# Tiles turned by one engine or another, GpSimd instructions of 256 columns, and who makes the lower parts during a tree of decays

## The chip, the cores and the metric

The program runs on one core of a Trainium2 chip. A core has TensorE (PE, matmuls and its weight loads, PEld), VectorE (DVE), ScalarE (ACT), GpSimd (POOL), and queues that move data; SyncE (SP) issues nearly all loads here. The metric is the device time of one launch, in microseconds (us). Engines execute their instructions in the order in which the program lists them, each waiting for the semaphores that its operands need.

## The reference, cut to what matters

Two layers. Each has two token mixers that run side by side and are merged (HGRN2, a gated recurrence, and stick-breaking attention), then a PEER layer: 8 heads choose 16 of 16,384 one-neuron experts for each of 256 tokens.

```
proj = (x * (1 + sc1) + sh1) @ w_in[l]
oa = hgrn2(qa, fa, ia)          # S_t = diag(f_t) S_{t-1} + (1 - f_t) outer v_t, o_t = S_t^T q_t
ob = stick_breaking_attention(qb, kb, vb)
merged = sigmoid(gate_a) * (norm(oa) * silu(ga) @ w_up_a[l]) + sigmoid(gate_b) * (ob @ w_up_b[l])
y = (merged @ w_o[l]) * gt1
x = layer_norm(DN_ALPHA * x + y, ln_g[l, 0], ln_b[l, 0])
hf = x * (1 + sc2) + sh2
idx, gates = product_key_top16(hf @ w_pq[l], sub_keys[l])
act = gelu(hf . peer_u[l][idx])
y = (sum over k of gates * act * peer_v[l][idx]) * gt2
x = layer_norm(DN_ALPHA * x + y, ln_g[l, 1], ln_b[l, 1])
```

The kernel computes the product of hf with all 16,384 rows of peer_u, and the product of the (mostly zero) gate matrix with all rows of peer_v.

## The kernel before

**Split products.** Every matrix that TensorE multiplies is split into an upper part (`wh`, rounded by ScalarE, the helper at L58) and a lower part (`wl` = raw minus wh, the subtraction at L271), and a product is three matmuls: upper by upper, upper by lower, lower by upper (the helper at L61). A tile of weights is 128 x 1024 numbers, so it has two upper halves and two lower halves of 512 columns each. `fetch` issues a load, `turn` does what a tile needs ahead of the split, `prep` splits it, `take` hands the oldest split tile to the matmuls and prepares the next. Instructions are listed in the order in which this Python code runs.

**Who makes the lower halves.** `lighter` keeps an estimate of the work listed on VectorE and GpSimd and picks the one with less for tiles of kind "w" (outside slabs) and "o"; expert tiles ("u", "x") have theirs on GpSimd (flag `pool_lo`/kind) while selection runs.

**Turning expert tiles.** The rows of `peer_u` have to stand with the model dimension on the partitions. A "u" tile is loaded by four DMAs in blocks of 32 and turned by one VectorE transpose of blocks (L220). An "x" tile is turned by eight TensorE transposes of 128x128 into PSUM (L251), from which ScalarE writes both the upper part and the plain copy. The table `uv_seq` (L124) makes every fourth tile with j under 100 an "x" tile.

**Stages of a layer.** Mixers, merge, layer norm, queries for PEER, then 126 tiles of `peer_u` (U stage) with the selection of the experts running beside them, then `peer_v` (V stage). In the U stage `pull(sides, budget)` lists a share of the selection's operations after each tile, by costs that the generators yield: `scores` and top-16 searches on VectorE, with the scores made by transposes and products on TensorE into the tile `G` and copied to SBUF by ScalarE (`buf<-G`).

**The tree over time.** `hgrn()` computes the recurrence over 256 steps as a tree of 9 levels (`sizes`). For a level `st_exp` lists two VectorE subtractions (L843, L844) and ScalarE's exponential, `st_mul` two VectorE products into `qk` (L856, L857), `st_score` TensorE's products (`hs`, `ss`), and `st_place` VectorE's masked copies into `sc` (L887). Between two levels a tile of weights for the projections is split and multiplied.

**Start of layer 1.** `make_masks()` (L684 and the lines around it) and `update_x()`, which finishes the layer norm of layer 0 by multiplying x by a row and adding one on GpSimd (L698, L702), run beside the first projections. In layer 0 the modulation sums `mh` (L381, L1143) stand there.

**The merge.** In the merge of the two mixers, tiles of w_o ("o") are scaled on GpSimd by `gt_row` in `turn` (L223), and VectorE adds the two gated parts (L1281 to L1283) and makes lower halves.

## Time and profile before

| | us |
|---|---|
| median of 3 runs | 2228.16 (2227.01 to 2228.52) |
| the profiled execution's own time | 2227.97 |
| its span in the trace | 2226.2 |
| PE busy | 2117.0 (95%) |
| DVE busy | 1819.4 (82%) |
| ACT busy | 1164.5 (52%) |
| POOL busy | 1063.8 (48%) |

The span is the time between the first and the last instruction in the trace; 1.8 us of the execution lie around it. Busy shares are means over stages with different limits. Layer 0 has its mixers in the first 300 us or so and its U stage from about 320 to 770; layer 1 starts near 1150 and has its U stage from about 1412 to 1862. In a row of a timeline, "x8" merges eight instructions in a row, the first number is the start, the second the time from the first start to the last end, and the bracket tells how long the engine was idle before it and what ended that.

### The profile page before, as it was taken

How to read it: one execution, taken by the hardware profiler on the slowest of the kernel's cores; microseconds unless marked ns; L12 is line 12 of the kernel's file. 1: busy time of each engine (PE TensorE's matmuls, PEld its weight loads, DVE VectorE, ACT ScalarE, POOL GpSimd, SP SyncE). 2: the span in 40 equal slices, each digit the busy share in tenths (PEclk: the TensorE clock that was granted, in tenths of full speed). 3: DMA queues.
4: the chain of work that ended last, by engine and by line, in shares of the span. 5: the costliest groups of instructions: out<-in, count | busy, mean ns of one | idle time of the engine just before them, and what ended most of it. 6: DMA issues, size and time to landing. Idle time of an engine off the chain costs nothing.

```text
span 2226.2 us, 42039 instructions
## 1 busy us (share of the span) xinstructions
PE 2117.0 (95%) x14484; PEld 1928.0 (87%) x14484; DVE 1819.4 (82%) x3296; ACT 1164.5 (52%) x2443; POOL 1063.8 (48%) x784
## 2 busy tenths in 40 slices
PE   5799899999999999999989998998999999999998
PEld 5789799999999977888779887998999999788886
DVE  7887979999999578888887658789999985766675
ACT  3446555545554545555545465555555545555562
POOL 4656637887778621000044534578877783300001
PEclk8899999999999999999999999999999999999999
DMA  8646567676665678888844335676766556666662
GB/s 281 193 133 221 167 132 158 149 151 146 143 147 146 186 251 270 282 283 284 298 153 146 120 103 146 149 155 142 154 146 145 147 159 192 220 196 191 197 226 87
DMA packets 448718, 400.30 MB, mean 180 GB/s; under 512 B 234576, under 2 KB 395896, under 8 KB 448504
## 3 DMA queue, kind: packets, MB, share of 16 engines
q1 hardware_dynamic: 446760, 392.33, 62.5%
q0 software_dynamic: 1408, 4.23, 0.6%
q8 instruction: 114, 1.87, 0.3%
q10 hardware_dynamic: 336, 1.06, 0.1%
q14 instruction: 100, 0.82, 0.1%
HBM read 396.46 MB, written 1.05 MB: 179 GB/s over the span
## 4 chain that ended last, share of the span: by engine, by line
PE 69%; DVE 15%; DMA 5%; issue 3%; ACT 3%; POOL 2%; SPq 1%; POOLq 0%; ACTq 0%; DVEq 0%
PE Y L61 27%; PE A L61 25%; PE T L61 7%; PE G L61 3%; DMA raw<-in_peer_u_dram 3%; POOL wl L271 2%; PE hs L61 2%; DVE wl L271 2%; PE ss L61 2%; PE T L251 2%; DMA raw<-in_peer_v_dram 1%; DVE qk L857 1%; DVE o L1512 1%; SPq L197 1%; DVE e L843 1%
## 5 line engine op out<-in xcount | busy, mean ns | idle before, releaser
L271 POOL TENSOR_TENSOR wl<-raw,wh 128x512 fp32r<-128x512 f32 x663 | 925.7, 1421 | 662.0 <-ACT wh L58 587.3
L58 ACT ACTIVATE wh<-raw 128x512 fp32r<-128x512 f32 x1088 | 627.7, 622 | 206.8 <-PE A L61 59.0
L61 PE MATMUL A<-hTh,wh 128*128 128x256 f32 x2080 | 538.5, 291 | 2.7 <-ACT wh L58 2.6
L61 PE MATMUL A<-hTl,wh 128*128 128x256 f32 x2080 | 521.0, 283 | 0.0
L61 PE MATMUL Y<-wh,o 128*128 128x512 f32 x1776 | 478.1, 391 | 0.5 <-DVE o L521 0.5
L271 DVE TENSOR_TENSOR wl<-raw,wh 128x512 fp32r<-128x512 f32 x525 | 379.7, 764 | 64.0 <-ACT wh L58 46.4
L61 PEld LDWEIGHTS A<-hTh,wh 128*128 128x128 f32 x2080 | 397.8, 191 | 4.7 <-ACT wh L58 4.0
L61 PEld LDWEIGHTS A<-hTl,wh 128*128 128x128 f32 x2080 | 398.7, 192 | 0.7
L61 PEld LDWEIGHTS Y<-wh,o 128*128 128x128 f32 x1776 | 332.6, 188 | 70.0 <-DVE o L521 0.9
L61 PE MATMUL A<-hTh,wl 128*128 128x256 f32 x2080 | 336.2, 284 | 13.5 <-POOL wl L271 13.4
L61 PEld LDWEIGHTS A<-hTh,wl 128*128 128x128 f32 x2080 | 286.9, 192 | 17.6 <-POOL wl L271 17.6
L61 PE MATMUL Y<-wl,o 128*128 128x512 f32 x888 | 276.3, 391 | 5.2 <-DVE wl L271 5.0
L220 DVE STREAM_TRANSPOSE raw<-raw 128x1024 f32<-128x1024 f32 x206 | 252.8, 1233 | 3.2 <-DMA raw<-in_peer_u_dram 2.7
L58 ACT ACTIVATE o<-buf 128x256 fp32r<-128x256 f32 x228 | 95.0, 417 | 272.6 <-PE Y L61 272.6
L521 DVE TENSOR_TENSOR o<-buf,o 128x256 fp32r<-128x256 f32 x228 | 100.7, 442 | 140.2 <-ACT o L58 140.2
L61 PEld LDWEIGHTS Y<-wl,o 128*128 128x128 f32 x888 | 167.1, 188 | 44.0 <-DVE wl L271 9.5
L58 ACT ACTIVATE buf<-G 128x128 f32<-128x128 f32 (+6 forms) x236 | 53.8, 273 | 202.7 <-PE G L61 202.7
L1507 DVE TENSOR_TENSOR o<-iT,iota_t 128x1024 f16<-128x1024 f16 x128 | 159.5, 1246 | 0.0
L570 POOL TENSOR_TENSOR x<-x,buf 128x1024 f32<-128x1024 f32 x1 | 2.4, 2392 | 280.9 <-DVE x L567 280.9
L1512 DVE TENSOR_TENSOR o<-gT,o 128x1024 f16<-128x1024 f16 x128 | 131.3, 1025 | 4.4
L61 PE MATMUL T<-hTh,wh 128*128 128x256 f32 x512 | 133.8, 293 | 0.0
L61 PE MATMUL T<-hTl,wh 128*128 128x256 f32 x512 | 130.4, 287 | 0.0
(496 smaller groups left out, 3212.6 us busy)
## 6 DMA issues: line engine op xcount, KB each, us to landing
raw<-in_peer_u_dram SPq DMA_DIRECT2D x1024, 128.0 KB, 3.5
raw<-in_peer_v_dram SPq DMA_DIRECT2D x256, 512.0 KB, 4.6
raw<-in_w_in_dram SPq DMA_DIRECT2D x88, 512.0 KB, 4.7
raw<-in_w_ada_dram SPq DMA_DIRECT2D x78, 512.0 KB, 4.9
raw<-in_w_o_dram SPq DMA_DIRECT2D x16, 512.0 KB, 3.5
raw<-in_w_pq_dram SPq DMA_DIRECT2D x64, 128.0 KB, 2.9
qk<-in_w_ada_dram SPq DMA_DIRECT2D x10, 512.0 KB, 3.7
e<-in_w_ada_dram SPq DMA_DIRECT2D x8, 512.0 KB, 6.0
```

Of the source, the lines that this page charges most:

```text
L58: nc.scalar.activation(o, i, f, **kw)
L61: nc.tensor.matmul(o, a, b, start=start, stop=stop, **kw)
L197: nc.sync.dma_start(dst[32 * b:32 * b + 32], src[b])
L220: nc.vector.transpose(t, t)
L251: nc.tensor.transpose(banks[s][:, q], t[:, (4 * s + q) * P:(4 * s + q + 1) * P], ident)
L271: eng.tensor_sub(lo, src, h.bitcast(F32))
L521: nc.vector.tensor_sub(lo, src, h.bitcast(F32))
L570: nc.gpsimd.tensor_mul(xt[tt], xt[tt], last[0])
L843: eng.tensor_sub(ev[:, :, :hn], mid, bv[:, :, :hn])
L857: nc.vector.tensor_mul(tv[:, :, hn:], nodes(qT, n)[:, :, hn:], ev[:, :, hn:])
L1507: nc.vector.tensor_tensor(o.rearrange("p a u n v -> p (a u) n v"), iT[:, b].rearrange("p a (u v) -> p (a u) v", v=2)[:, :, None] .to_broad ...
L1512: nc.vector.tensor_mul(og.rearrange("p u a n v -> p (u a) n v"), gT[:, b * nu:(b + 1) * nu].rearrange("p u a v -> p (u a) v")[:, :, None] ...
```

## The change

Three things change.

First, an "x" tile now needs 24 <= j < 100, so j = 3, 7, 11, 15, 19 and 23 of each layer become "u" tiles: other DMAs, one VectorE transpose in place of eight of TensorE, and one ScalarE pass over the tile in place of two. In the first 24 tiles the budget of `pull` is 1.75 after every tile; before it was 1.55, and 2.75 after an "x" tile.

Second, GpSimd's 128x512 subtractions for tiles other than "u" and "x" become two of 256 columns, its multiply of an "o" tile by `gt_row` four of 256 (counted as 2.9 in the planner's estimate, before 2.4), and the four 128x1024 operations of `update_x` sixteen of 256, with one listed for each step of the side work.

Third, from the start of `hgrn()` to the end of its loop over levels, a flag makes VectorE do every lower half that GpSimd might have got, without adding it to the planner's estimate.

```diff
-    uv_seq = [("x" if j % 4 == 3 and j < 100 else "u", j) for j in range(NK)] + [("v", j) for j in range(NK)]
+    uv_seq = [("x" if j % 4 == 3 and 24 <= j < 100 else "u", j) for j in range(NK)] + [("v", j) for j in range(NK)]
...
             elif kind == "o" and state.get("gt_row") is not None:
-                nc.gpsimd.tensor_mul(t, t, state["gt_row"])
-                load["pool"] += 2.4
+                for c in range(0, 1024, 256):
+                    nc.gpsimd.tensor_mul(t[:, c:c + 256], t[:, c:c + 256], state["gt_row"][:, c:c + 256])
+                load["pool"] += 2.9
                 fetched[i] = ("ot", t)
...
             else:
-                eng = lighter(0.6, 1.0) if kind == "o" or kind == "w" and not state.get("slab") else nc.vector
-            eng.tensor_sub(lo, src, h.bitcast(F32))
+                eng = nc.vector if state.get("vector_lo") else lighter(0.6, 1.0) if kind == "o" or kind == "w" and not state.get("slab") else nc.vector
+            if kind not in "ux" and eng is nc.gpsimd:
+
+                for c in (slice(0, 256), slice(256, 512)):
+                    eng.tensor_sub(lo[:, c], src[:, c], h[:, c].bitcast(F32))
+            else:
+                eng.tensor_sub(lo, src, h.bitcast(F32))
...
-                for tt in range(2):
-                    nc.gpsimd.tensor_mul(xt[tt], xt[tt], g_row)
-                    load["pool"] += 2.4
-                    yield None
-                    yield None
-                    nc.gpsimd.tensor_add(xt[tt], xt[tt], b_row)
-                    load["pool"] += 2.4
-                    yield None
+                for n in range(16):
+                    cs = slice(n % 4 * 256, n % 4 * 256 + 256)
+                    xc = xt[n // 8][:, cs]
+                    (nc.gpsimd.tensor_add if n // 4 % 2 else nc.gpsimd.tensor_mul)(
+                        xc, xc, (b_row if n // 4 % 2 else g_row)[:, cs])
+                    load["pool"] += 0.7
                     yield None
...
+                state["vector_lo"] = True
                 sc0 = ap.tile([P, HG_H, S], F32, name="sc0")
...
+                state["vector_lo"] = False
                 fine[0] = l == 1
...
-                    pull(sides, 1.55 + 1.2 * (kind == "x"))
+                    pull(sides, 1.75 if j < 24 else 1.55 + 1.2 * (kind == "x"))
```

Lines from L223 on have other numbers in the changed file: the subtraction at L271 is L277 (in pieces, L275), L843/L844 are L849/L850, L856/L857 are L862/L863, L887 is L893, L698/L702 are L706, and the row loads at L434 are L440.

On VectorE, in one level of the tree of layer 1, before (two exponent subtractions, two masked copies, two products, and the next level's subtractions):

```order
L843 TENSOR_TENSOR e<-bb 128x128x4
L844 TENSOR_TENSOR e<-bb 128x128x4
L887 COPY_PREDICATED sc_14338<-masks,hs 128x4x4x16
L887 COPY_PREDICATED sc_14339<-masks,ss 128x16x16
L856 TENSOR_TENSOR qk<-kk,e 128x128x4
L857 TENSOR_TENSOR qk<-qT,e 128x128x4
```

and one level in the changed kernel:

```order
L849 TENSOR_TENSOR e<-bb 128x32x16
L850 TENSOR_TENSOR e<-bb 128x32x16
L277 TENSOR_TENSOR wl<-raw,wh 128x512 x2
L893 COPY_PREDICATED sc_14403<-masks,hs 128x4x64
L893 COPY_PREDICATED sc_14404<-masks,ss 128x4x64
L862 TENSOR_TENSOR qk<-kk,e 128x32x16
L863 TENSOR_TENSOR qk<-qT,e 128x32x16
```

Two lower halves now stand on VectorE between the level's subtractions and its copies and products. On ScalarE, at the same place of the changed kernel, the order is as before: the level's exponential, then the two upper halves that those lower halves are made from.

```order
L58 ACTIVATE e<-e 128x1024
L58 ACTIVATE wh<-raw 128x512 x2
L58 ACTIVATE sc_14403<-hs 128x4x128
L58 ACTIVATE e<-e 128x1024
L58 ACTIVATE wh<-raw 128x512 x2
```

Nothing moved on ScalarE there. On GpSimd, at the start of layer 1, before (`mh` are the two rows of the layer norm):

```order
L434 DMA mh_13854<-in_ln_g_dram 128x1024
L434 DMA mh_13855<-in_ln_b_dram 128x1024
L271 TENSOR_TENSOR wl<-raw,wh 128x512 x2
L698 TENSOR_TENSOR x_79<-x_79,mh_13854 128x1024
L271 TENSOR_TENSOR wl<-raw,wh 128x512
L702 TENSOR_TENSOR x_79<-x_79,mh_13855 128x1024
L271 TENSOR_TENSOR wl<-raw,wh 128x512
```

and in the changed kernel:

```order
L440 DMA mh_13897<-in_ln_g_dram 128x1024
L440 DMA mh_13898<-in_ln_b_dram 128x1024
L275 TENSOR_TENSOR wl<-raw,wh 128x256 x4
L706 TENSOR_TENSOR x_79<-x_79,mh_13897 128x256
L275 TENSOR_TENSOR wl<-raw,wh 128x256 x2
L706 TENSOR_TENSOR x_79<-x_79,mh_13897 128x256
L275 TENSOR_TENSOR wl<-raw,wh 128x256 x2
```

The same data pass through GpSimd in quarters and halves, and one quarter of an x operation now alternates with one 512-column half made of two pieces.

On TensorE, in the first 24 expert tiles, eight transposes stand between the products of two tiles before:

```order
L61 MATMUL A<-hTh,wl 128x256 x4
L61 MATMUL K<-buf_3125,buf_3124 128x256
L251 MATMUL T<-ident,raw 128x128 x8
L61 MATMUL A<-hTh,wh 128x256
L61 MATMUL A<-hTl,wh 128x256
```

In the changed kernel the row of eight transposes is gone there, six times in each layer; the first one stands after tile 24. VectorE has a transpose of its own in their place.

## Rows read from the trace of the kernel before

**Rows 1.** Busy time of each engine in stretches: the first 80 us of the U stage of layer 0, a later part of it, and the first 80 us of the U stage of layer 1. The columns are the stretch, its length, then for PE, PEld, DVE, ACT and POOL the busy us with the number of instructions, the granted TensorE clock, DMA share and GB/s.

```profile
322.70:402.60 79.90, 79.90 (x652) 79.05 (x651) 69.48 (x371) 46.25 (x102) 60.17 (x49) 1.00 0.72 158
475.00:690.00 215.00, 213.64 (x1989) 208.88 (x1988) 210.27 (x303) 118.30 (x312) 166.55 (x118) 1.00 0.64 148
1416.40:1496.30 79.90, 79.90 (x652) 79.06 (x651) 69.48 (x371) 46.25 (x102) 60.16 (x49) 1.00 0.72 158
```

**Rows 2.** What VectorE waits for in the first stretch of rows 1: total us, times, longest.

```profile
DVE buf L1404 <- ACT G L58: 10.4, 8, 2.4
```

**Rows 3.** The timeline of TensorE at one "x" tile of that stretch.

```profile
342.33 1.03 PE L251 MATMUL T<-ident,raw 128*128 128x128 f32 x8
343.12 0.36 PE L61 MATMUL A<-hTh,wh 128*128 128x256 f32 x1
```

**Rows 4.** VectorE's transposes in that stretch, by line: count, busy us, mean ns.

```profile
L220 DVE STREAM_TRANSPOSE raw<-raw 128x1024 f32<-128x1024 f32 x17 | 21.0, 1238 | 0.0
```

**Rows 5.** The timeline of VectorE in one level of the tree of layer 1.

```profile
1228.65 0.68 DVE L844 TENSOR_TENSOR e<-bb 128x512 f32<-128x512 f32 x1
1229.26 0.43 DVE L887 COPY_PREDICATED sc<-masks,hs 128x256 f32<-128x256 uint8 x1
1229.59 0.44 DVE L887 COPY_PREDICATED sc<-masks,ss 128x256 f32<-128x256 uint8 x1
1230.52 0.69 DVE L856 TENSOR_TENSOR qk<-kk,e 128x512 f32<-128x512 f32 x1 [0.49 <-ACT e L58]
1231.13 1.79 DVE L857 TENSOR_TENSOR qk<-qT,e 128x512 f32<-128x512 f32 x1
1232.84 1.75 DVE L843 TENSOR_TENSOR e<-bb 128x512 f32<-128x512 f32 x1
1234.51 0.68 DVE L844 TENSOR_TENSOR e<-bb 128x512 f32<-128x512 f32 x1
```

**Rows 6.** ScalarE in the same level.

```profile
1229.43 1.06 ACT L58 ACTIVATE e<-e 128x1024 f32<-128x1024 f32 x1 [3.29 <-DVE e L844]
1230.39 1.14 ACT L58 ACTIVATE wh<-raw 128x512 fp32r<-128x512 f32 x2
```

**Rows 7.** GpSimd in the same level.

```profile
1231.09 2.96 POOL L271 TENSOR_TENSOR wl<-raw,wh 128x512 fp32r<-128x512 f32 x2 [2.90 <-ACT wh L58]
```

**Rows 8.** VectorE in level 0 of the tree of layer 0: a modulation sum.

```profile
107.16 1.28 DVE L381 SCALAR_TENSOR_TENSOR acc<-raw,cond,acc 128x1024 f32<-128x1024 f32 x1
```

**Rows 9.** What TensorE waits for in the tree of layer 0 and, below it, in that of layer 1: total us, times, longest.

```profile
PE hs L61 <- DVE qk L857: 11.9, 7, 6.5
...
PE hs L61 <- DVE qk L857: 7.7, 7, 1.8
```

**Rows 10.** GpSimd over the whole run by line and shape: the product with gt_row, and the only form of 256 columns.

```profile
L223 POOL TENSOR_TENSOR raw<-raw,gt_row 128x1024 f32<-128x1024 f32 x16 | 43.0, 2694 | 3.0 <-DVE gel L1283 1.6 <-DVE v_a L271 1.3
L1737 POOL TENSOR_TENSOR x<-x,buf 128x256 f32<-128x256 f32 x32 | 30.6, 991 | 4.7 <-DMA buf<-in_ln_b_dram 4.7
```

**Rows 11.** GpSimd at the start of layer 1.

```profile
1159.03 2.55 POOL L271 TENSOR_TENSOR wl<-raw,wh 128x512 fp32r<-128x512 f32 x2
1163.60 2.41 POOL L698 TENSOR_TENSOR x<-x,mh 128x1024 f32<-128x1024 f32 x1 [2.02 <-DMA mh<-in_ln_g_dram]
```

**Rows 12.** VectorE at the start of layer 1: operations on the masks, then lower halves.

```profile
1158.16 3.46 DVE L684 TENSOR_TENSOR m_a<-m_a,m_b 128x4 f32<-128x4 f32 x1
...
1162.20 0.17 DVE L684 TENSOR_TENSOR m_a<-m_a,m_b 128x8 f32<-128x8 f32 x1
...
1163.74 2.32 DVE L684 TENSOR_TENSOR m_a<-m_a,m_b 128x32 f32<-128x32 f32 x1
...
1167.20 2.38 DVE L682 TENSOR_SCALAR m_a<-iota_f,part_f 128x64 f32<-128x64 f32 x1
...
1170.18 3.70 DVE L271 TENSOR_TENSOR wl<-raw,wh 128x512 fp32r<-128x512 f32 x6
```

**Rows 13.** TensorE at the start of layer 1.

```profile
1170.93 1.23 PE L61 MATMUL T<-hTh,wl 128*128 128x256 f32 x4 [4.87 <-DVE wl L271]
```

**Rows 14.** VectorE at the start of layer 0: eight modulation sums, and eight again with GpSimd idle.

```profile
41.49 5.28 DVE L381 SCALAR_TENSOR_TENSOR mh<-e,cond,mh 128x256 f32<-128x256 f32 x8
...
61.43 3.25 DVE L381 SCALAR_TENSOR_TENSOR mh<-e,cond,mh 128x256 f32<-128x256 f32 x8
```

**Rows 15.** GpSimd at the start of layer 0.

```profile
43.64 4.26 POOL L271 TENSOR_TENSOR wl<-raw,wh 128x512 fp32r<-128x512 f32 x3 [2.11 <-ACT wh L58]
...
54.50 6.34 POOL L271 TENSOR_TENSOR wl<-raw,wh 128x512 fp32r<-128x512 f32 x5
```

**Rows 16.** VectorE in the merge of layer 1.

```profile
1341.26 2.89 DVE L1283 TENSOR_TENSOR gel<-gel,mgb 128x512 f32<-128x512 f32 x1
...
1349.37 2.89 DVE L1283 TENSOR_TENSOR gel<-gel,mgb 128x512 f32<-128x512 f32 x1
1352.18 3.45 DVE L271 TENSOR_TENSOR wl<-raw,wh 128x512 fp32r<-128x512 f32 x2
```

**Rows 17.** What TensorE waits for: at the start of layer 0, in the merge of layer 0, and in the merge of layer 1.

```profile
PE ss L61 <- DVE mh L1143: 8.5, 2, 4.4
...
PE T L61 <- DVE wl L271: 2.4, 2, 1.8
...
PE T L61 <- DVE wl L271: 4.9, 2, 2.8
```

## The prediction

> **What bounds the kernel now.** I read the busy shares first: PE works 95% of the span, so most of the time is matmul work that the change leaves alone, and a gain has to come out of the few stretches in which PE waits, or out of work taken from PE. Then I read windows. In the first 80 us of the U stage PE has no gap at all, 79.90 of 79.90 us, while DVE is busy 69.48 [rows 1]; DVE's 10.4 us of idle there are one wait, for ScalarE's copy of scores that PE makes in its turn [rows 2]. So there DVE waits for PE. Later in the stage PE has 213.64 of 215.00 us and DVE 210.27 [rows 1], so both are close to full. In the two trees over time it is the other way round: PE waits 11.9 and 7.7 us for VectorE's products [rows 9]. At the start of layer 0 PE waits 8.5 us for modulation sums, at the start of layer 1 4.87 us for a lower half, and in the merges 2.4 and 4.9 us for lower halves [rows 13, 17]. All of these last waits are on DVE. The sum goes against the profiled execution, 2227.97 us, 0.19 below the median.
>
> **A, the tiles not turned by TensorE.** Six tiles a layer lose eight transposes each. From their start to that of the next matmul is 343.12 - 342.33 = 0.79 us [rows 3], so PE loses 6 x 0.79 = 4.7 us a layer, in a stretch where it sets the pace; 79.9 becomes 75.2. DVE gains 6 x 1.238 = 7.4 us [rows 4]. The budget of the side work in these 24 tiles goes from 24 x 1.55 + 6 x 1.2 = 44.4 to 24 x 1.75 = 42.0, so 2.4 us of selection leave the stretch. DVE is then busy 69.48 + 7.4 - 2.4 = 74.5 us of 75.2. That fits only if its wait of 10.4 us [rows 2] shrinks to 0.7. It should shrink nearly so: DVE waits since it is ahead of PE, and a slower DVE with a faster PE is less ahead. Of 4.7 I count 4.0 as gained. The 2.4 us that are moved later meet a DVE that is nearly full [rows 1]. Most of the stage after them has PE in front, and the selection ends some tiles before the U stage does, so I charge 0.7 and not 2.4. That leaves 3.3 a layer. Layer 1's stretch reads the same to 0.01 us [rows 1], so A is -6.6. Bounds: -9.4 (all of 2 x 4.7) and 0, where the moved work and the waits eat it; the case beyond 0 is the first rival. The loads are four DMAs of 128 KB a tile in either kind, on the same queue, with a DMA share of 0.72 in the stretch [rows 1], and ScalarE, 46.25 us busy of 79.9, loses a pass: both at nothing, with that slack as their cover.
>
> **C, lower halves in the tree by VectorE.** The change frees DVE from GpSimd and gives it GpSimd's work. In a level before, the second product and the next subtraction take 1.79 and 1.75 us in place of about 0.69, exactly while GpSimd makes its two lower halves [rows 5, 7]: 2 x 1.08 = 2.2 us to be saved. The two halves cost 2 x 0.60 (spacing of uncontended operations, 1228.65 to 1229.26 and 1230.52 to 1231.13 [rows 5]). By that alone a level would go from 5.86 (1228.65 to 1234.51 [rows 5]) to 4.9. But the halves stand in DVE's order before the copies and products, and their upper halves stand on ScalarE behind the level's exponential: 1.06 us, then two of about 0.55 [rows 6]. GpSimd could start them at 1231.09, which is 2.44 us after the second subtraction began [rows 5, 7]; DVE can't sooner. Behind DVE's wait are queued the two copies, the two products, and for them PE. The chain from one second subtraction to the next becomes 2.44 + 2 x 0.60 (halves) + 2 x 0.33 (copies, 1229.26 to 1229.59 [rows 5]) + 2 x 0.60 (products) + 0.60 (next first subtraction) = 6.10: 0.24 more than now. The first three of the seven steps have no copies: 5.44, 0.42 less. In the last level the products end 2.44 + 1.20 + 0.66 + 1.20 = 5.5 after the subtraction, now 1232.84 - 1228.65 = 4.2: 1.3 more. Layer 1: 4 x 0.24 - 3 x 0.42 + 1.3 = +1.0. In layer 0 two of the steps without copies hold a modulation sum of 1.2 us [rows 8], which now runs inside the wait and would run after the halves: 2 x (6.64 - 5.86) - 0.42 + 4 x 0.24 + 1.3 = +3.4. Together +4.4. Bounds: +8 (0.2 more in each of 16 levels, where an upper half comes later than GpSimd's start shows) and -13.1, all that PE waits inside the two trees, (11.9 - 6.5) + 7.7 [rows 9]; the 6.5 lies ahead of the first level.
>
> **B, GpSimd in pieces of 256.** From 512 columns at 2.55 / 2 = 1.27 us and 1024 at 2.41 [rows 11], a straight line gives 0.14 us for each instruction and 0.70 for 256 columns. The one form of 256 in the trace takes 0.99 [rows 10]; it is of another loop, beside busy neighbours, so I take 0.70 and keep 0.99 as an end. A DVE operation on two SBUF operands waits while a GpSimd one runs: the sum L1283 took 2.89 us behind a multiply with gt_row (mean 2.69) [rows 10, 16], and a mask product 2.32 behind an x operation where the same line takes 0.17 free [rows 11, 12]. With pieces such a wait is 0.7.
>
> The Trainium skill, "SBUF — State Buffer", section "Who interferes with whom", says that the two engines share one port pair as an exclusive lock held for a whole instruction, and that a VectorE instruction with two SBUF inputs contends with GpSimd's reads. The waits in the tree and in the merge agree [rows 5, 16]. The wait of 3.46 us at 1158.16 [rows 12] went through two GpSimd instructions of 1.27 in a row [rows 11], which a lock freed after each would not give; by the lock alone the term for that place would be some 1.2 us larger.
>
> What it is worth depends on how dense DVE's own work is. Merges: DVE has one sum and two lower halves behind each multiply. The first sum would begin 0.7 instead of 2.2 us late, and the first lower half after it, which PE waits for, some 0.85 us earlier; at 1349.37, where two multiplies follow each other and the sum and the halves take 2.89 and 3.45 [rows 16], I find the first half done 2.5 us earlier. With about half of layer 0's 2.4 us [rows 17] that is 0.85 + 2.5 + 0.7, about -4.0 of the 7.3 waited. Start of layer 1: DVE loses 2.15 and 2.14 us to the x operations at 1163.74 and 1167.20 [rows 12], plus about 1 to the half between them; six mask operations that remain would each meet one piece, 6 x 0.70 = 4.2 for 5.2 now: -1.2 of PE's 4.87 [rows 13]. Start of layer 0: eight modulation sums take 5.28 beside GpSimd and 3.25 free [rows 14], and behind five halves in a row [rows 15] ten pieces meet DVE operations one by one, each 0.70, where five of 1.27 did: +0.7. The layer norms and what runs ahead of the trees: -0.5. B is -4.0 - 1.2 + 0.7 - 0.5 = -5.0. Bounds: if every DVE wait shrinks as its GpSimd instruction does, by 1 - 0.70/1.27 = 45% at the start of layer 0 and 1 - 0.70/2.41 = 71% in the merges and the start of layer 1, it is 0.45 x 8.5 + 0.71 x (4.87 + 2.4 + 4.9) = -12.5; if nothing shrinks and GpSimd itself comes late, the x operations take 16 x 0.70 - 4 x 2.41 = 1.6 longer and ten halves of the first tiles 0.13 each: about +3 (with 0.99 a piece, +6).
>
> **Sum:** -6.6 + 4.4 - 5.0 = -7.2, so 2220.8 us.
>
> **Rivals.** First, on the other side: the waits of DVE for scores stay in the first 24 tiles. They are waits for an answer of PE and ScalarE to something DVE made a while before; if this delay is one of queues, DVE needs 69.48 + 7.4 - 2.4 + 10.4 = 84.9 us where the stretch takes 79.9, and each layer loses 5.0. It decides from the point where more than 5.4 of the 10.4 us stay. With B and C as above: +10.0 + 4.4 - 5.0 = +9.4, 2237.4. For it: VectorE is the engine that gets work where it is 87% busy. Against: 79.90 of 79.90 on PE says that now nothing waits for DVE there, and the longest wait is 2.4 us, less than one tile's time.
>
> Second, the tree comes free. If lower halves don't wait behind the exponential, PE's waits within the trees go: -13.1 for +4.4, in all -24.7, 2203.3. For it: DVE's own work in a level is 4.9. Against: ScalarE's order, which the change leaves.
>
> Third, pieces gain nothing. GpSimd moves the same columns, so DVE is kept off for the same time, in more and shorter parts, and each piece costs 0.14 more: B is +2.0 and the total -6.6 + 4.4 + 2.0 = -0.2, 2227.8, no change. For it: at both starts DVE lists operations on SBUF densely, and usually one gets through between two GpSimd instructions. Against: the merges, with few such operations. The page named above says that one holds the pair and the other blocks fully, by which the blocked time is only divided; the trace has no row that divides it.
>
> Fourth, A's gain is lost in the selection's later part, with B and C as forecast: -0.6, 2227.4.
>
> **How the numbers follow.** 46% for the forecast, 13% for the first rival, 10% for the second, 23% for the third, 8% for the fourth. A measurement of this kernel can tell about 0.2% from no change, 4.5 us. The forecast lies 2.7 us beyond that and its terms are uncertain by some 4, so about 36 of its 46 are faster, 9 the same and 1 slower; the second rival is faster, and 4 of the third's 23. Faster 36 + 10 + 4 = 50%, same 9 + 18 + 8 = 35%, slower 13 + 2 = 15% with what the bounds of C and B allow. The range goes from the second rival, 2203, to 2233, which C's +8 and B's +3 with A's -6.6 (+4.4, 2232.4) reach; it leaves out the first rival and a few per cent of tails.
>
> **What would show it.** A: the first 24 tiles take 75 to 76 us with DVE's wait for scores under 2; at 80 or more, the first rival. C: levels of the tree 6.1 us apart, with DVE idle until ScalarE's upper halves; at under 5.0 the second rival. B: in the merges the sum L1283 at 1.4 us and no wait of PE over 1 us; at both starts about the same waits as now, and if the merges too keep theirs, the third rival. The forecast is wrong most easily in A, if DVE at 74.5 of 75.2 us can't be kept that full.

## The result and the profile after

| | before | changed |
|---|---|---|
| median | 2227.75 us (4 runs, 2227.01 to 2228.52) | 2212.16 us (4 runs, 2210.43 to 2214.30) |
| ratio | | 0.993 (95% interval 0.9913 to 0.9948) |
| profiled execution, own time / span | 2227.97 / 2226.2 | 2214.30 / 2212.5 |

The changed kernel is 15.6 us faster by the medians; 7.2 were forecast. The time is in the range, the sign is right, and the forecast gain is a little under half of the measured one. So the question is which terms were too small.

TensorE has 13,893 matmuls at L61 in every one of these kernels, most of them in the same order, so the start of the n-th can be compared all along the program. The table gives, at the ends of stages, by how many us it starts later (+) or earlier (-) than in the kernel before, for the changed kernel and for the experiments told below. (In brackets: the time in the kernel before. The first matmul of all starts 0.7 to 0.8 us late in the profiled runs of the changed kernel, of "first part" and of "budget alone", a difference in the first loads. At the end of the tree of layer 1 the n-th matmul of "break moved" is another one, so that entry is good to 2 us only.) The columns are of the profiled executions, which lie up to 2.5 us from the medians: 2214.30 us for the changed kernel (median 2212.16), 2200.91 for "break moved" (median 2203.43), 2223.52 for "budget alone" (median 2221.46).

| end of stage | changed | first part | second part | third part | first and second | break moved | budget alone |
|---|---|---|---|---|---|---|---|
| start of layer 0 (95.6) | -0.7 | +1.2 | -1.3 | +0.0 | -1.1 | -2.5 | +1.0 |
| tree of layer 0 (165.6) | +1.8 | +1.4 | -5.6 | +3.0 | -5.3 | -2.4 | +0.7 |
| merge and norm (324.1) | +1.2 | +0.7 | -6.1 | +3.1 | -5.8 | -2.1 | -0.1 |
| first 24 expert tiles (403.7) | -4.0 | -4.5 | -6.1 | +3.1 | -11.0 | -7.4 | -0.0 |
| U stage (769.3) | -6.3 | -5.8 | -6.9 | +2.1 | -13.3 | -9.6 | -3.6 |
| V stage and norm (1153.5) | -7.4 | -6.7 | -7.5 | +2.9 | -14.3 | -12.7 | -3.2 |
| masks of layer 1 (1183.9) | -12.8 | -6.3 | -11.4 | +3.1 | -19.7 | -18.7 | -2.4 |
| tree of layer 1 (1271.1) | -8.1 | -6.3 | -14.5 | +2.7 | -19.5 | -20.6 | -2.4 |
| merge and norm (1401.0) | -7.8 | -6.6 | -14.5 | +2.7 | -20.3 | -20.2 | -2.4 |
| first 24 expert tiles of layer 1 (1496.3) | -13.1 | -11.8 | -14.5 | +2.7 | -25.5 | -25.4 | -2.4 |
| U stage (1847.8) | -13.5 | -13.6 | -14.5 | +2.5 | -27.0 | -26.9 | -4.3 |
| end (2198.5) | -13.7 | -13.8 | -14.8 | +2.2 | -27.1 | -27.1 | -4.5 |

**The first expert tiles.** The stretch of the changed kernel between the same matmuls as the first of [rows 1], and DVE's wait that answers to [rows 2]; columns as there:

```profile
323.90:398.60 74.70, 74.70 (x604) 73.94 (x603) 73.07 (x369) 41.59 (x90) 59.50 (x48) 1.00 0.61 165
```

```profile
DVE buf L1411 <- ACT G L58: 1.5, 2, 1.4
```

PE still has no gap, and DVE's wait for scores went from 10.4 us to 1.5: DVE filled up, 73.07 us of 74.70 (forecast 74.5 of 75.2). The stretch gained 5.2 us in the table (from +1.2 to -4.0), and the stage as a whole 7.5.

**The tree.** One level of the changed kernel's layer 1 on VectorE, and ScalarE beside it, for [rows 5, 6]:

```profile
1218.67 0.68 DVE L850 TENSOR_TENSOR e<-bb 128x512 f32<-128x512 f32 x1
1221.05 1.29 DVE L277 TENSOR_TENSOR wl<-raw,wh 128x512 fp32r<-128x512 f32 x2 [1.71 <-ACT wh L58]
1222.27 0.44 DVE L893 COPY_PREDICATED sc<-masks,hs 128x256 f32<-128x256 uint8 x1
1222.60 0.43 DVE L893 COPY_PREDICATED sc<-masks,ss 128x256 f32<-128x256 uint8 x1
1222.93 0.68 DVE L862 TENSOR_TENSOR qk<-kk,e 128x512 f32<-128x512 f32 x1
1223.53 0.68 DVE L863 TENSOR_TENSOR qk<-qT,e 128x512 f32<-128x512 f32 x1
1224.13 0.68 DVE L849 TENSOR_TENSOR e<-bb 128x512 f32<-128x512 f32 x1
1224.73 0.68 DVE L850 TENSOR_TENSOR e<-bb 128x512 f32<-128x512 f32 x1
```

```profile
1219.44 1.06 ACT L58 ACTIVATE e<-e 128x1024 f32<-128x1024 f32 x1 [3.49 <-DVE e L850]
1220.41 1.14 ACT L58 ACTIVATE wh<-raw 128x512 fp32r<-128x512 f32 x2
```

No operation is held up by GpSimd any longer (each takes 0.68), but DVE is idle for 1.71 us until ScalarE has an upper half, which stands behind the exponential. From one L850 to the next it is 6.06 us, where 6.10 was forecast and 5.86 was before.

**The start of layer 1.** PE's wait of 4.87 us [rows 13] is gone, and the table shows -5.4 there. But it doesn't last. VectorE and GpSimd in the decays ahead of the tree, and PE at its first products:

```profile
1181.20 3.07 DVE L809 TENSOR_SCALAR f_z<-f_z,lb 128x256 f32<-128x256 f32 x4
1184.19 1.22 DVE L277 TENSOR_TENSOR wl<-raw,wh 128x512 fp32r<-128x512 f32 x1
1185.33 4.43 DVE L816 TENSOR_SCALAR kk<-kk,lb 128x256 f32<-128x256 f32 x4
1189.69 1.22 DVE L277 TENSOR_TENSOR wl<-raw,wh 128x512 fp32r<-128x512 f32 x1
```

The last of the four `kk` operations by itself:

```profile
1187.59 2.18 DVE L816 TENSOR_SCALAR kk<-kk,lb 128x256 f32<-128x256 f32 x1
```

```profile
1184.08 1.94 POOL L275 TENSOR_TENSOR wl<-raw,wh 128x256 fp32r<-128x256 f32 x2
1185.97 0.79 POOL L706 TENSOR_TENSOR x<-x,mh 128x256 f32<-128x256 f32 x1
1186.73 1.54 POOL L275 TENSOR_TENSOR wl<-raw,wh 128x256 fp32r<-128x256 f32 x2
1188.20 0.95 POOL L831 MEMSET sc<- 128x1024 f32 x1
1189.10 0.52 POOL L832 MEMSET sc<- 128x512 f32 x1
```

```profile
1195.44 0.74 PE L61 MATMUL T<-hTh,wl 128*128 128x256 f32 x4 [1.27 <-DVE wl L277]
1201.38 2.08 PE L61 MATMUL hs<-qk 128*128 128x128 f32 x8 [3.77 <-DVE qk L863]
```

The sixteen pieces of x are now listed one by one as far as the decays, so GpSimd is busy there without a gap, with pieces of halves, a piece of x and two memsets, and the four `kk` operations take 4.43 us: the first three 0.83 each, the last 2.18, until GpSimd's second memset is done. The kernel before has this row, with GpSimd idle:

```profile
1197.21 1.13 DVE L812 TENSOR_SCALAR kk<-kk,lb 128x256 f32<-128x256 f32 x4
```

PE then waits 1.27 and 3.77 us, and of the 5.4 us that the masks gave 1.9 are left at the first products of the tree and 0.7 at its end. This loss hangs on where the operations fall, and not on the pieces as such: with the second part alone (below), `kk` falls into a gap of GpSimd, and the 3.9 us gained there stay.

```profile
1187.01 1.13 DVE L816 TENSOR_SCALAR kk<-kk,lb 128x256 f32<-128x256 f32 x4
```

**The merges.** L1283's first 2.89 us [rows 16] are 0.69 now (1.4 was forecast), and PE's waits for lower halves on T went from 4.9 to 1.7 us in layer 1 [rows 17]:

```profile
1333.34 0.69 DVE L1290 TENSOR_TENSOR gel<-gel,mgb 128x512 f32<-128x512 f32 x1
1333.94 2.38 DVE L277 TENSOR_TENSOR wl<-raw,wh 128x512 fp32r<-128x512 f32 x2
```

```profile
PE T L61 <- DVE wl L277: 1.7, 2, 1.2
```

Yet the table has little gain from merge and norm in either layer (0.6 us and a loss of 0.3). One reason is that other short waits came up: over this merge and norm, PE's longer waits summed to 7.7 us before and are 6.3 now. The other is the clock. Three stretches of the changed kernel (columns as in [rows 1]; the last column but two is the granted clock):

```profile
1342.00:1350.00 8.00, 6.46 (x48) 5.88 (x47) 8.00 (x8) 4.63 (x9) 8.00 (x8) 1.00 0.52 156
1350.00:1360.00 10.00, 7.76 (x33) 5.62 (x32) 9.23 (x12) 5.68 (x9) 10.00 (x11) 1.00 0.55 154
1360.00:1375.00 15.00, 13.38 (x36) 8.82 (x37) 11.00 (x19) 4.17 (x8) 6.40 (x6) 0.66 0.76 164
```

PE was busy 6.46 of 8 and 7.76 of 10 us at the full clock, and then the granted clock fell to 0.66 over 15 us, which means part of it at the lower of the two levels, 1.2 GHz. The same matmuls, first in the changed kernel, then in the kernel before:

```profile
1369.49 0.63 PE L61 MATMUL ss<-qbT,acc 128*128 128x512 f32 x1
1369.92 0.63 PE L61 MATMUL ss<-qbT,mh 128*128 128x512 f32 x1
```

```profile
1377.64 0.39 PE L61 MATMUL ss<-qbT,acc 128*128 128x512 f32 x1
1377.87 0.40 PE L61 MATMUL ss<-qbT,mh 128*128 128x512 f32 x1
```

They follow each other by 0.43 us and by 0.23. Up to 1361.15 us the changed kernel had gained 4.2 us in the stage; the next fifteen matmuls took 9.2 us, 1.4 of it short waits, where the kernel before took 4.7. That gives it back.

The low clock is not new, though: the kernel before has it inside the merge, right behind each of PE's two waits for lower halves.

```profile
1340.00:1350.00 10.00, 7.89 (x54) 7.69 (x54) 9.64 (x13) 5.67 (x11) 5.54 (x4) 0.83 0.62 185
1350.00:1360.00 10.00, 7.18 (x48) 6.98 (x47) 10.00 (x7) 4.80 (x9) 8.20 (x4) 0.83 0.43 132
```

There some sixteen matmuls of 256 columns follow each other by 0.21 us and not 0.12, after either wait; in the changed kernel these run at 0.12. So about 3 us of what the merge had gained by then were the clock's, and in the main the change moved the low clock from the merge to the stretch behind it, where there is more of it (0.66 over 15 us, against 0.83 over two times ten).

### The profile page after: what moved, and what is told of

It is laid out like the page before. It is cut to its first block, busy times and chain, and to the rows that moved or that the text cites. A ratio compares the mean times of both kernels' runs of the same rounds, so it can differ in the third digit from the quotient of the medians.

```text
span 2212.5 us, 42041 instructions
## 1 busy us (share of the span) xinstructions
PE 2107.0 (95%) x14388; PEld 1913.3 (86%) x14388; DVE 1791.7 (81%) x3357; ACT 1153.1 (52%) x2417; POOL 1071.2 (48%) x923
## 5 line engine op out<-in xcount | busy, mean ns | idle before, releaser
L277 POOL TENSOR_TENSOR wl<-raw,wh 128x512 fp32r<-128x512 f32 x512 | 721.5, 1435 | 179.3 <-ACT wh L58 138.1
L58 ACT ACTIVATE wh<-raw 128x512 fp32r<-128x512 f32 x1112 | 640.4, 622 | 229.1 <-POOL wl L277 58.3
L61 PE MATMUL A<-hTh,wh 128*128 128x256 f32 x2080 | 538.8, 291 | 3.1 <-ACT wh L58 3.0
L61 PE MATMUL A<-hTl,wh 128*128 128x256 f32 x2080 | 521.2, 283 | 0.0
L277 DVE TENSOR_TENSOR wl<-raw,wh 128x512 fp32r<-128x512 f32 x570 | 402.2, 745 | 99.8 <-ACT wh L58 81.9
L61 PE MATMUL Y<-wh,o 128*128 128x512 f32 x1776 | 477.9, 391 | 0.9 <-DVE o L527 0.5
L275 POOL TENSOR_TENSOR wl<-raw,wh 128x256 fp32r<-128x256 f32 x212 | 178.4, 872 | 495.3 <-ACT wh L58 494.3
L61 PEld LDWEIGHTS A<-hTh,wh 128*128 128x128 f32 x2080 | 398.1, 191 | 5.1 <-ACT wh L58 4.3
L61 PEld LDWEIGHTS A<-hTl,wh 128*128 128x128 f32 x2080 | 398.9, 192 | 0.8
L61 PEld LDWEIGHTS Y<-wh,o 128*128 128x128 f32 x1776 | 332.8, 188 | 70.5 <-ACT wh L58 1.5
L61 PE MATMUL A<-hTh,wl 128*128 128x256 f32 x2080 | 336.3, 284 | 10.3 <-POOL wl L277 10.0
L61 PEld LDWEIGHTS A<-hTh,wl 128*128 128x128 f32 x2080 | 286.9, 192 | 14.4 <-POOL wl L277 14.2
L61 PE MATMUL Y<-wl,o 128*128 128x512 f32 x888 | 276.3, 391 | 4.8 <-DVE wl L277 4.6
L220 DVE STREAM_TRANSPOSE raw<-raw 128x1024 f32<-128x1024 f32 x218 | 266.9, 1229 | 4.3 <-DMA raw<-in_peer_u_dram 3.8
L61 PEld LDWEIGHTS Y<-wl,o 128*128 128x128 f32 x888 | 166.9, 188 | 43.3 <-DVE wl L277 8.4
L58 ACT ACTIVATE buf<-G 128x128 f32<-128x128 f32 (+4 forms) x232 | 52.6, 270 | 196.6 <-PE G L61 196.6
L1514 DVE TENSOR_TENSOR o<-iT,iota_t 128x1024 f16<-128x1024 f16 x128 | 151.5, 1183 | 0.0
L1519 DVE TENSOR_TENSOR o<-gT,o 128x1024 f16<-128x1024 f16 x128 | 137.0, 1070 | 4.4
L61 PE MATMUL T<-hTh,wh 128*128 128x256 f32 x512 | 131.9, 290 | 0.0
```

The costliest lines, as they stand in the source:

```text
L58: nc.scalar.activation(o, i, f, **kw)
L61: nc.tensor.matmul(o, a, b, start=start, stop=stop, **kw)
L220: nc.vector.transpose(t, t)
L275: eng.tensor_sub(lo[:, c], src[:, c], h[:, c].bitcast(F32))
L277: eng.tensor_sub(lo, src, h.bitcast(F32))
L1514: nc.vector.tensor_tensor(o.rearrange("p a u n v -> p (a u) n v"), iT[:, b].rearrange("p a (u v) -> p (a u) v", v=2)[:, :, None] .to_broad ...
```

## The experiments

**The three parts alone.** Each run undoes the others in the changed kernel, that is, the diff shown ahead of the prediction is applied only in the named part.

First part: the table of tiles and the budget.

```diff
+    uv_seq = [("x" if j % 4 == 3 and 24 <= j < 100 else "u", j) for j in range(NK)] + ...
+                    pull(sides, 1.75 if j < 24 else 1.55 + 1.2 * (kind == "x"))
```

> The kernel before with the first part alone (no tiles turned by TensorE among the first 24, budget 1.75). Theory, from the trace of the changed kernel: a tile not turned on TensorE gives 0.87 us (5.2 us in the first 24 tiles of layer 0), twelve tiles 10.4, and the later part of the selection adds 1 to 2 us of gain where the prediction charged a loss of 1.4: about -12, so 2215 to 2217. Rival, the prediction's own size: -6.6, 2221. If the tiles' gain were lost later in the selection: 2226 to 2228.

Measured: 2214.42 us against 2227.66, ratio 0.9943 (0.9929 to 0.9956): -13.2. The theory's size, a little more. The gain is in the U stages: -6.5 us in layer 0 and -7.1 in layer 1.

Second part: the pieces (L223, L271, `update_x`).

```diff
+                for c in (slice(0, 256), slice(256, 512)):
+                    eng.tensor_sub(lo[:, c], src[:, c], h[:, c].bitcast(F32))
```

> The kernel before with the second part alone (GpSimd's work in pieces of 256 columns). Theory: the waits of TensorE that go at the start of layer 1 (about 5 us) and in the merges (about 4 us each) are given back before the next stage, at the decays ahead of the tree and in a stretch of low granted clock behind the merges, so that only the start of layer 0 (2 to 3 us) is left: 2224 to 2226. Rival: the local gains stay, -10 or more, 2218 or less. Second rival, pieces only divide the blocked time: 2227 to 2229.

Measured: 2213.17 us, ratio 0.9933 (0.992 to 0.9947): -14.5. My theory was wrong, and so is the second rival that pieces only divide the blocked time. But the gain isn't where the first rival wanted it: merge and norm together give 0.5 us in layer 0 and 0.1 in layer 1. It comes from the start of layer 0 (-1.3), the two trees (-4.2 and -3.1) and the start of layer 1 (-3.9).

Third part: the flag in `hgrn()`.

```diff
+                state["vector_lo"] = True
...
+                state["vector_lo"] = False
```

> The kernel before with the third part alone (VectorE makes all lower halves during the tree). Theory: levels 6.1 us apart in place of 5.86, and 3 to 4 us lost, nearly all in layer 0: 2230 to 2232. Rival: the tree is freed of GpSimd's port and the time falls, 2215 to 2224. By the theory a wait of VectorE for the upper halves stands in each level; by the rival it doesn't.

Measured: 2228.65 us, ratio 1.0007 (0.9998 to 1.0016): +1.0, less than expected and not told from no change; the profiled run has +3.0 in the tree of layer 0 and -0.4 in that of layer 1. The -0.4 are -1.5 ahead of the first products and +1.2 over the levels, which are up to 6.07 us apart with a wait of VectorE of about 1.7 in each, as the theory has it. The loss in all is below the theory's, and the rival's gain isn't there. The sum of the three parts alone is -13.2 - 14.5 + 1.0 = -26.7, and the changed kernel has -15.6: 11 us are lost where two parts meet.

**First and second part, without the third.**

```diff
-                state["vector_lo"] = True
-                state["vector_lo"] = False
```

> The changed kernel without its third part (the planner divides the lower halves in the tree, GpSimd's in two pieces of 256). Theory: the third part costs 3 to 4 us, nearly all in layer 0, so this is faster than the changed kernel: 2207 to 2210. Rival: the third part pays or is free, 2212 or more.

Measured: 2200.58 us, ratio 0.9877 (0.9862 to 0.9892): -27.1, and 11.6 us faster than the changed kernel. The first two parts add up to within 0.6 us. The third part costs three times what I expected on top of them. In the tree with GpSimd's halves in pieces, one level on VectorE and GpSimd beside it:

```profile
1207.86 0.69 DVE L861 TENSOR_TENSOR qk<-kk,e 128x512 f32<-128x512 f32 x1 [0.49 <-ACT e L58]
1208.47 1.25 DVE L862 TENSOR_TENSOR qk<-qT,e 128x512 f32<-128x512 f32 x1
1209.64 1.23 DVE L848 TENSOR_TENSOR e<-bb 128x512 f32<-128x512 f32 x1
1210.79 1.21 DVE L849 TENSOR_TENSOR e<-bb 128x512 f32<-128x512 f32 x1
...
1213.19 0.69 DVE L861 TENSOR_TENSOR qk<-kk,e 128x512 f32<-128x512 f32 x1 [0.49 <-ACT e L58]
```

```profile
1208.43 4.17 POOL L275 TENSOR_TENSOR wl<-raw,wh 128x256 fp32r<-128x256 f32 x4 [0.47 <-ACT wh L58]
```

A level takes 5.33 us (1207.86 to 1213.19), 0.53 less than before. Three operations wait about 0.55 each, 1.6 in all, where two waited 1.1 each [rows 5]. GpSimd waits in its turn, with 4.17 us for four pieces. Its fourth piece falls beside VectorE's two masked copies, which take 0.43 and 0.44 us as before. The third part puts 6.06 in the place of that 5.33.

The Trainium skill, "SBUF — State Buffer", section "Who interferes with whom", has the shared ports held for a whole instruction. The single waits agree, with 0.55 us behind a piece and 1.1 behind a half. But the time that is lost isn't fixed by the columns that GpSimd moves: 2.2 us a level with halves, 1.6 with pieces.

**Where VectorE's halves stand in the tree.** The changed kernel with the break between two steps of the side work moved, so that the two halves stand behind the level's products:

```diff
-                    yield 2.4
+                    yield None
                     if i < n:
                         st_exp(i)
-                    yield None
+                    yield 2.4
```

> The changed kernel with one edit in the tree: the break between two steps of the side work stands behind the exponent's operations no longer but ahead of them, so that VectorE's two lower halves stand behind the level's products and not ahead of its copies and products. Theory: the third part costs time only since the halves make the products wait for upper halves that stand behind the exponential on ScalarE; put behind the products, a level is 1.87 us to the products, 1.2 for them, 1.2 for the halves and 0.6 for the next subtraction, 4.9 us in place of 6.15 in the changed kernel: 14 steps, 13 to 18 us faster than the changed kernel, 2195 to 2199. Rival: VectorE's added work or TensorE's own bounds the level at 5.3 or more: 2201 or more.

Measured: 2203.43 us (2200.91 to 2206.36), ratio 0.9895 (0.988 to 0.991): 8.7 faster than the changed kernel, less than expected. (The profile is of the fastest of its four executions, 13.4 us under the profiled one of the changed kernel.) Its levels are as computed, 4.90 us from the first row here to the last:

```profile
1206.40 0.69 DVE L862 TENSOR_TENSOR qk<-kk,e 128x512 f32<-128x512 f32 x1 [0.50 <-ACT e L58]
1207.01 0.68 DVE L863 TENSOR_TENSOR qk<-qT,e 128x512 f32<-128x512 f32 x1
1207.62 1.29 DVE L277 TENSOR_TENSOR wl<-raw,wh 128x512 fp32r<-128x512 f32 x2
1208.82 0.69 DVE L849 TENSOR_TENSOR e<-bb 128x512 f32<-128x512 f32 x1
1209.42 0.68 DVE L850 TENSOR_TENSOR e<-bb 128x512 f32<-128x512 f32 x1
...
1211.30 0.69 DVE L862 TENSOR_TENSOR qk<-kk,e 128x512 f32<-128x512 f32 x1 [0.50 <-ACT e L58]
```

So the third part's cost within a level is the place of the halves and not VectorE's added work. Something is lost ahead of the first products, where PE waits 8.3 us in layer 0 and 6.0 in layer 1, against 5.4 and 3.8 in the changed kernel; whether that is all that is missing to the expectation is not shown.

**The first level back in its place.** As above, with no break ahead of the first level and the flag set from the second level on:

```diff
-                state["vector_lo"] = True
...
-                    yield None
+                    if i:
+                        state["vector_lo"] = True
+                        yield None
```

> All three parts, with the halves behind the level's products as in the run with the moved break, but with no break ahead of the first level's exponent and with the flag set only from the second level on. Theory: the moved break held levels at 4.9 us, but put a tile's work ahead of the first level in layer 0 (5 us late there, 1 us in layer 1); without that, 4 to 7 us less than that run's 2203.4: 2196 to 2200, as fast as or faster than the first two parts alone. Rival: the late first level was set by the decays and not by the break: 2202 to 2204.

Measured: 2205.78 us (2201.62 to 2206.24), ratio 0.9901 (0.9886 to 0.9916). The rival, or somewhat worse; with spreads of 5 us the two runs can't be told apart. In the profiles, the tree of layer 0 begins 5.6 us earlier than in the run above and ends 3.6 earlier, but by the count of matmuls PE gains 0.5 of it at the end of that stage: its longest wait for products is still 6.8 us. VectorE's earlier tree didn't help it, and I don't know what list of work ahead of the first level would.

**What in the pieces counts.** First and second part, each time with one of the three kinds of pieces whole again.

```diff
+                nc.gpsimd.tensor_mul(t, t, state["gt_row"])
+                load["pool"] += 2.4
...
```

> First and second part, with the product with gt_row whole again (1024 columns). Theory: the pieces there earn about 4 us in each merge, which are given back right behind it in a stretch of lower granted clock, so no change against the first two parts together: 2199 to 2202. Rival: they earn what the waits showed, 2207 to 2209 without them.

Measured: 2199.64 us, ratio 0.9872 (0.9857 to 0.9887), 0.9 under the run with pieces: no difference, as the theory has it. With pieces the granted clock is 0.66 for ten us behind the merge of layer 1 (first row). Without them it is 1.00 there (second row), but 0.83 over ten us inside the merge, behind PE's wait (third row):

```profile
1348.00:1358.00 10.00, 7.47 (x17) 4.32 (x18) 8.01 (x12) 4.47 (x8) 7.00 (x7) 0.66 0.58 132
```

```profile
1348.00:1358.00 10.00, 7.42 (x29) 5.06 (x30) 8.85 (x12) 4.80 (x9) 4.16 (x4) 1.00 0.72 169
1330.00:1340.00 10.00, 6.01 (x39) 5.81 (x38) 9.93 (x11) 4.79 (x9) 8.28 (x5) 0.83 0.43 159
```

```diff
+                for tt in range(2):
+                    nc.gpsimd.tensor_mul(xt[tt], xt[tt], g_row)
...
+                    nc.gpsimd.tensor_add(xt[tt], xt[tt], b_row)
```

> First and second part, with the layer norm's end (update_x) in four operations of 1024 again. Theory: the masks at the start of layer 1 wait again for whole operations, TensorE waits nearly 5 us for a lower half, and 3 to 5 us are lost: 2203 to 2206. Rival: the decay chain ahead of the tree sets that stage's end either way: 2200 to 2201.

Measured: 2201.37 us, ratio 0.9879 (0.9864 to 0.9895): 0.8 over the run with pieces, no difference. My theory was wrong and the rival right: the masks come later with whole operations, PE's matmuls behind them by 5.6 us (-14.1 in place of -19.7 at the table's seventh row), and by the end of the tree both are at the same place (-19.3 and -19.5).

```diff
-                for c in (slice(0, 256), slice(256, 512)):
-                    eng.tensor_sub(lo[:, c], src[:, c], h[:, c].bitcast(F32))
```

> First and second part, with lower halves on GpSimd whole again (512 columns). Theory: the halves in pieces are what shortened the tree, 5.33 us a level in place of 5.86, about 3 us in each layer, and some 2 us at the start of layer 0: 2207 to 2210 without them. Rival: the pieces of x and gt_row carry the gain: 2200 to 2203.

Measured: 2209.22 us, ratio 0.992 (0.9907 to 0.9934): 8.6 lost, as expected. The halves in pieces carry the second part: 5.7 us up to the end of the tree of layer 0, and 4.7 from the start of layer 1 to the end of its tree, of which a part is given back later.

**What in the first part counts.** The tiles with the old budget, on the kernel before:

```diff
-                    pull(sides, 1.55 + 1.2 * (kind == "x"))
+                    pull(sides, 1.55 + 1.2 * (j % 4 == 3 and j < 100))
```

> The kernel before with the tiles of the first part but the side work's budget as before (2.75 after j = 3, 7 and so on, 44.4 us in the first 24 tiles). Theory: the gain is the transposes' (0.87 us a tile on TensorE), VectorE is full with 69.5 + 7.4 = 76.9 us in the first 24 tiles where TensorE needs 74.7, so some 2 us a layer of the 5.2 are lost there and none later: -8 to -10, 2218 to 2220. Rival: the budget doesn't matter, as with the first part whole: 2213 to 2216.

Measured: 2220.38 us, ratio 0.9966 (0.9952 to 0.9979): -7.6, about what the theory has. The budget matters: with it, the same tiles gain 13.2.

The budget alone, with the tiles turned as before:

```diff
-                    pull(sides, 1.55 + 1.2 * (kind == "x"))
+                    pull(sides, 1.75 if j < 24 else 1.55 + 1.2 * (kind == "x"))
```

> The kernel before with the budget of the first part alone (1.75 after every one of the first 24 tiles, which are turned as before). Theory: TensorE sets the pace there, so nothing in the first 24 tiles, and 2.4 us of selection moved later cost up to 1 us a layer: 2227 to 2230. Rival: the later start of the selection's decoding is where the unforeseen 1 to 2 us a layer come from: 2224 to 2226.

Measured: 2221.46 us, ratio 0.9972 (0.9962 to 0.9982): -6.5, more than even the rival expected; with the -7.6 of the tiles that is about the first part's 13.2. Nothing changes in the first 24 tiles; the gain lies behind them, most of it in the next 75 us of each U stage, where the selection's results are decoded (3.5 and 1.9 us in the profile, to the end of the U stage). PE's waits from 400 to 478 us, with this budget:

```profile
PE A L61 <- POOL wl L271: 4.5, 6, 1.3
```

The kernel before has, from 402 to 475 us:

```profile
PE A L61 <- POOL wl L271: 6.6, 9, 1.5
```

The same 44.4 us as before, spread evenly:

```diff
+                    pull(sides, 1.85 if j < 24 else 1.55 + 1.2 * (kind == "x"))
```

> The kernel before with a budget of 1.85 after every one of the first 24 tiles: 24 x 1.85 = 44.4 us, the amount of before, evenly spread and not in bursts of 2.75 (the tiles are turned as before). Against the run with 1.75 alone, which gained 6.5 us. First theory, the amount: the gain comes from 2.4 us of selection being moved past tile 24, so this is as before, 2227 to 2229. Second theory, the place: it comes from where the selection's long operations fall among the tiles of the next stretch, which the spreading moves too: any other time, up to 3 us a layer, so 2221 to 2225 or over 2230.

Measured: 2225.24 us (11 runs), ratio 0.9986 (0.9977 to 0.9995): -2.9, between the ranges of the two theories, at the edge of the second. In the profile, which is of the slowest of the eleven (2227.15) and has gained 0.8 us, PE waits there as long as before:

```profile
PE A L61 <- POOL wl L271: 6.5, 8, 1.5
```

So both count: 2.9 of the 6.5 us come with the spreading alone, and the other 3.6 with the smaller amount of selection ahead of tile 24. With intervals of about 2 us on either number, the runs don't tell which is the larger.

## Why the prediction was right in its sign and range, and half in its size

**A, forecast -6.6, measured alone -13.2.** The mechanism in the first 24 tiles was right: PE's transposes were on the path, DVE's wait for scores shrank (to 1.5 us, forecast 0.7), and the first rival didn't come. Two terms were mis-sized. One is the transposes. A tile gives 0.87 us and not 0.79: 5.2 us in six tiles, of which I had counted 4.0. The time from the first transpose to the next matmul left out what the following matmul of rows 3, 0.36 us long in place of 0.28, still carried. The other is the step that failed: "The 2.4 us that are moved later meet a DVE that is nearly full ... so I charge 0.7". The sign was wrong, and with it the fourth rival. Behind the first 24 tiles the first part gains another 1.3 us in layer 0 and 1.8 in layer 1, and the budget alone 3.5 and 1.9; I had charged a loss of 0.7 in each. On top of the tiles the budget is worth 5.6 us in all (13.2 less 7.6): partly behind the first 24 tiles, and partly in them, where with the old budget the tiles gain only 3.7 and 3.4 us of the 5.2. I had not looked at what binds the stretch behind them: PE waits 6.6 us there for GpSimd's lower halves. With the budget alone it waits 4.5 us, in the changed kernel 4.8. That the wait falls is shown; how so small a shift of the selection does it is not: it can be the place of VectorE's long operations among GpSimd's halves, and no run shows that.

**C, forecast +4.4, measured alone +1.0, and on top of A and B +11.6.** The chain was right to 0.04 us (6.06 for 6.10), and so was its cause, since halves behind the products give 4.90. Against the tree of before the cost is small, as computed: in layer 0 +3.4 forecast and +3.0 seen, in layer 1 +1.0 forecast and +1.2 seen over the levels (with -1.5 ahead of the first products, which the forecast didn't have). What failed is the step that both C and B were measured against the level of before, 5.86 us. The second part alone would have made it 5.33. I listed the pieces at the two starts, in the merges and the layer norms, and left out the tree, since in the changed kernel GpSimd has no lower halves there. For the changed kernel's own time that is right, and it is why the sum of B and C came out near: together they are the changed kernel less the first part, -15.6 + 13.2 = -2.4, forecast -0.6. For what each part is worth it was wrong.

**B, forecast -5.0.** By places, in the changed kernel: start of layer 0 +0.7 forecast, -1.5 seen (-0.7 in the table less the late first load). PE's two waits there were 4.01 and 4.45 us and are 2.7 and 5.2: the second got longer as computed, the first shorter, and the rest of the gain lies ahead of both. Merges -4.0 forecast: the waits for lower halves fell as computed, by about 3 us in layer 1, and the time didn't, for the other waits that came up and for the clock, which is low behind the merge now and no longer in it. I had worked out a wait and called it time, without asking what comes behind it. Start of layer 1 -1.2 forecast: -5.4 at the masks, since I let too many mask operations meet a piece, and then given back in the decays to -1.9 at the first products. The small number was near the truth by luck; with the second part alone it is -3.9. One of my bounds was also added up wrongly: the +6 for pieces of 0.99 us holds the x operations alone, and with the ten halves it would be about +13. Pieces that met no wait took between 0.7 and 0.8 us.

**The rivals.** The second, the free tree, is refuted for the changed kernel: the order on ScalarE does what I said. With the halves behind the products it comes true within the levels. The third, pieces gain nothing, holds on top of the first part for two kinds of pieces (x and gt_row, each within 1 us) and is refuted for the halves (8.6 us).

The first two parts without the third, 2200.58 us, beat both kernels; with gt_row whole it is 2199.64, not to be told from it. The run with the break moved, 2203.43 us with a fastest execution of 2200.91, is not clearly slower either.

## What to carry to other kernels

A part that takes work from an engine and a part that makes the same work cheaper there are not worth their sum: cost each against the kernel with the other. When a wait on the path goes, follow the next stage to its end before calling it gain; in the changed kernel most of what the waits at the masks and in the merges gave was paid back within 30 us. And when work is moved later, look at what binds the stretch that receives it, and not at how full one engine is there.

## What was not expected of the hardware

The granted clock took back what shorter waits gave. In the merge of layer 1, the kernel before has a granted clock of 0.83 twice, over ten us each, behind PE's two long waits. With the pieces the clock is 1.00 in the merge, and 0.66 over 15 us behind it, where the matmuls follow each other by 0.43 us in place of 0.23. With gt_row whole on top of the first two parts it is low in the merge again and 1.00 behind it, and the end is the same.

Four VectorE operations of 128x256 with a scalar operand, 1.13 us with GpSimd idle, took 4.43 beside it: 0.83 each for the first three, behind one piece of 256 columns each, and 2.18 for the fourth, which came through only when a piece and two memsets of GpSimd were done.
